# A hybrid decoder step: who issues the recurrence's small loads, and where its triangular solve pauses

## The chip, the cores and the metric

The kernel runs on one core of a Trainium2 chip. The metric is the device time of one execution in microseconds (us); the time of a kernel is the median of its runs.

## The reference

One inference step of a two-layer trunk over a prompt of 16 + 2048 positions and over 8 sequences of 4 new tokens. Layer 0 is sliding-window attention, layer 1 is RWKV-7 time mixing; each has a SiLU gate and a residual, and a last RMSNorm ends the step. The change lies in layer 1, whose core is a recurrence over tokens, for 16 heads with a 64 x 64 state each:

```
def wkv_scan(S0, r, w, k, v, a, b):
    # S_t = S_{t-1} diag(w_t) + (S_{t-1} a_t) b_t^T + v_t k_t^T ;  y_t = S_t r_t
    def step(S, inp):
        r_t, w_t, k_t, v_t, a_t, b_t = inp
        sa = jnp.einsum('bhvk,bhk->bhv', S, a_t)
        S = S * w_t[:, :, None, :] + sa[..., None] * b_t[:, :, None, :] + v_t[..., None] * k_t[:, :, None, :]
        return S, jnp.einsum('bhvk,bhk->bhv', S, r_t)
    S, ys = lax.scan(step, S0, xs)
...
    y = ((y - mean) * lax.rsqrt(var + GN_EPS)).reshape(B, T, R_WIDTH)
    y = y * ln_g.astype(f32) + ln_b.astype(f32)
    y = (y + bonus.reshape(B, T, R_WIDTH)) * jax.nn.silu(g.astype(f32))
    out = jnp.einsum('btw,wd->btd', y.astype(xn.dtype), w_out)
```

## The kernel before

The work stands in three stages: attention, the projections of layer 1, and the recurrence with its output. The change is in the third.

**Units and chunks.** The recurrence goes over units: unit 0 holds the 16 meta tokens (one chunk of 32), units 1 to 16 hold 128 prompt tokens in 4 chunks of 32, and the sample rows come last. Inside a chunk the token-by-token recurrence is turned into matrix products: a small triangular system is solved for every head, and the state moves on once a chunk. `chain` is the serial part of a chunk, in this order: TensorE multiplies Z (the state and the chunk's rows of v) by L into bank C; ScalarE copies the product to `R0s`; TensorE multiplies by `TT`, the inverted triangles (`solve`); ScalarE copies the result into Z; TensorE multiplies Z by the keys `LS`; VectorE scales by the decay products `pe` and writes the next chunk's Z, from which the next chunk's first product is taken.

**What a unit needs two units ahead.** For unit s = u + 2, `scores` makes 32 x 32 triangles on TensorE in two banks, in chunk 1 and in chunk 2 of u. ScalarE copies the triangles out of the banks to `LAs`; VectorE masks the rest of the banks back into `L`. `inverse` then writes `LAs` to a DRAM buffer `la_d`, reads it back with one triangle a row (`LA`), and inverts the triangles column by column on GpSimd: two tensor_tensor, `XT` and `X`, for each of 31 columns j. The result goes out to `tt_d`, and `load_TT` reads it back as `TT`.

**What runs beside it.** `project_out` of unit u - 2 (chunks 0, 1) and `gate` of unit u - 1 (chunks 2, 3) are dense products in steps that fill TensorE between the links of the chain. `outputs` (Y) reads two chunks' Z in one go, in chunk 2 and in chunk 0 of the next unit. `group_norm` is VectorE and ScalarE work with one power on GpSimd (`var`, in chunk 0); `project_out` has one too (`ms`, in chunk 2). 

**Order.** From unit 2 on, `in_order` fixes the order on VectorE, ScalarE and GpSimd as the one in which the program names the instructions; TensorE and SyncE (SP) are ordered by a list scheduler that works with modelled times and priorities. `released` puts a block's instructions behind the last link of the chain on each engine that stands in `anchors`. `inverse` is a generator: at each `yield` it stops, and `steady` takes it on in the next chunk; so its pauses say which GpSimd work of the norms comes between which columns. SP issues nearly all DMAs, in its own order, and stands still before one whose buffer is not free.

**Buffers.** Four Z buffers turn round, chunk by chunk; `pe` and `bont` (decay products and bonus factors of a unit) have four buffers each in the third stage's pool `wk`, which lies where earlier stages had their work tiles; `wp` is a pool that lasts from the second stage to the end.

Of the kernel before, what the change touches and what calls it, by code (L numbers as in the profile page):

```python
# [19 lines left out]
P = 128  # L20
D = 1024
KC = 8
# [8 lines left out]
def tile_hybrid_step(ctx: ExitStack, tc: tile.TileContext, a, o, c):  # L31
# [14 lines left out]
    def stt(out, in0, scalar, in1, op0, op1):  # L46
        v_.scalar_tensor_tensor(out=out, in0=in0, scalar=scalar, in1=in1, op0=op0, op1=op1)  # L47

    def dma(out, in_):
        return nc.sync.dma_start(out=out, in_=in_).ins  # L50

    cst = ctx.enter_context(tc.tile_pool(name="cst", bufs=1))
    dram = ctx.enter_context(tc.tile_pool(name="dram", bufs=1, space=DRAM))
# [889 lines left out]
    def scores(u, c2):  # L943

        nch = u.nch
        mk = smk_s if u.kind == "s" else smk
        w = min(2, nch - 2 * c2)
        L = u.L[c2]

        pss = banks(u)  # L950
        for g in range(KC):
            for cc in range(w):
                for e, ps_ in HS:
                    u.scored = mm(pss[e][64 * cc:64 * cc + 64, g, :], u.BK[g // 4][ps_, g % 4, 2 * c2 + cc, :], L[ps_, e, cc, g, :], True, True)
        for cc in range(w):
            r0 = 64 * cc
            for e in range(2):
                la = u.LAs[32 * (1 - e):32 * (1 - e) + 32, :, 2 * c2 + cc]
                sc = pss[e][r0:r0 + 32, :, 0:32].rearrange("p (h g) i -> p h g i", h=2)
                if u.kind == "s":  # L960
                    for half in range(2):
                        tt(v_, la[:, half], sc[:, half], smk_a[r0:r0 + 32, None, :].broadcast_to([32, 4, 32]), ALU.mult)
                else:
                    act(la, sc)
        for cc in range(w):
            r0 = 64 * cc
            for e in range(2):
                tt(v_, L[OS[e], e, cc], pss[e][r0:r0 + 64], mk[r0:r0 + 64, None, :].broadcast_to([64, KC, 64]), ALU.mult)

    def inverse(u, room=None, ln=None):  # L970

        nch = u.nch
        nl = nch * 16
        la_d = dramr.tile([2, nl // 2, 32, 32], F32, name="la_d", tag=f"la_d{nch}")
        u.tt_d = tt_d = dramr.tile([32, 4, 4 * nch * 32], F32, name="tt_d", tag=f"tt_d{nch}")
        for e in range(2):
            dma(la_d[e].rearrange("l j i -> j l i"),
                u.LAs[32 * e:32 * e + 32].rearrange("p h c g i -> p (h c g) i"))
        eng = v_ if u.idx == 1 else g_
        if u.kind == "m":  # L980
            room = wl.tile([P, 2, 32 * 32], F32, name="roomm", tag="L", bufs=nbuf["L"])
        if room is not None:
            LA = room[:, 0].rearrange("p (j i) -> p j i", i=32)
            XX = room[:, 1].rearrange("p (a k i) -> p a k i", a=2, i=32)
        else:

            LA = wk.tile([P, 32, 32], F32, name="LA", tag="LA", bufs=2)
            XX = None
        if XX is None:
            X = wk.tile([P, 16, 32], F32, name="X", tag="X", bufs=2)  # L990
            XT = wk.tile([P, 16, 32], F32, name="XT", tag="XT")
        else:
            X, XT = XX[:, 0], XX[:, 1]
        if ln is None:
            ln = wp.tile([P, 32], F32, name="ln", tag=("mu", "rst0")[u.idx % 2])
        if nch < 4:
            g_.memset(LA, 0.0)
            g_.memset(ln, 1.0)
        for hh in range(2):
            dma(LA[hh * 64:hh * 64 + nl], la_d.rearrange("e l j i -> (e l) j i"))  # L1000
            dma(ln[hh * 64:hh * 64 + nl], ln_d[u.idx].rearrange("q c g i -> (q c g) i"))
        tt(eng, LA, LA, ln.unsqueeze(2).broadcast_to([P, 32, 32]), ALU.mult)
        dma(X, c["laneid"])

        low = 16 if u.kind == "m" else 0

        part = {2: 16}.get(u.idx, 0)
        cut = [(v_, 0, part), (g_, part, 16)] if 0 < part < 16 else [(v_, 0, 16)] if part else [(eng, 0, 16)]
        for j in range(low, 31):
            if j in (8, 16, 23):  # L1010
                yield
            w = 3 - j % 4 if u.kind == "s" else 31 - j
            for eng, k0, k1 in cut if w else ():
                ks = slice(max(low // 2, k0), min(j // 2 + 1, k1))
                shape = [P, ks.stop - ks.start, w]
                if shape[1] <= 0:
                    continue
                tt(eng, XT[:, ks, :w], LA[:, j:j + 1, j + 1:j + 1 + w].broadcast_to(shape), X[:, ks, j:j + 1].broadcast_to(shape), ALU.mult)
                tt(eng, X[:, ks, j + 1:j + 1 + w], X[:, ks, j + 1:j + 1 + w], XT[:, ks, :w], ALU.add)
        for eng, k0, k1 in reversed(cut):  # L1020
            u.inverted = tt(eng, X[:, k0:k1], X[:, k0:k1], ln[:, None, :].broadcast_to([P, k1 - k0, 32]), ALU.mult)
        for hh in range(2):
            dma(tt_d[hh:32:2].rearrange("k q (l i) -> (q l) k i", i=32), X[hh * 64:hh * 64 + nl])
# [238 lines left out]
    with ExitStack() as ph:  # L1262
# [50 lines left out]
        def small_loads(u):  # L1313
            if u.kind == "s":
                room = wp.tile([P, 192], F32, name="TTs", tag="l1_0")
                u.TT = room[:, 0:128].rearrange("p (c g i) -> p c g i", c=1, i=32)
                u.pe = room[:, 128:192].rearrange("p (g c) -> p g c", c=8)
            else:
                u.pe = wk.tile([P, KC, u.nch], F32, name="pe", tag="pe", bufs=4)
            dma(u.pe, pe_d[u.idx])  # L1320
            if u.kind != "m":
                u.bont = wk.tile([P, 16], F32, name="bont", tag="bont", bufs=4)
                dma(u.bont[:u.n], bo_d[u.idx])

        def new_LAs(u):
# [2 lines left out]
        def load_TT(u):  # L1328
            if u.kind != "s":
                u.TT = wp.tile([P, u.nch, 4, 32], F32, name="TT", tag=("sels", "l2t")[u.idx % 2])  # L1330
            for gh in range(2):
                dma(u.TT[64 * gh:64 * gh + 64].rearrange("p c g i -> p (c g i)"), u.tt_d[:, gh:4:2].rearrange("k q x -> q k x"))
# [17 lines left out]
        anchors = {}  # L1350
        MARK = -1

        def new_Z(u, ch):

            Z = Zs[Zcount[0] % nbuf["Z"]]
            Zcount[0] += 1
            for e in range(2):
                load_v(u, ch, e, Z)
            return Z

        def load_v(u, ch, e, Z):
            b0, r0 = OS[e].start, u.off + ch * 32
            anchors["SP"] = dma(Z[b0 + 32:b0 + 64, e].rearrange("p g d -> p (g d)"), v_d[u.t][r0:r0 + 32, e, :])

        LScount = [0]
        over = []
# [47 lines left out]
        def chain(u, ch):  # L1414
# [15 lines left out]
            anchors["PE"] = m  # L1430
            anchors["ACT"] = act(R0s, C[0][:, 0])

            if ch + 1 < u.nch:
                Zn = new_Z(u, ch + 1)
                u.Z.append(Zn)
            elif u.next is not None:
                Zn = new_Z(u.next, 0)
                u.next.Z.append(Zn)
            else:
                Zn = None  # L1440
# [315 lines left out]
        def steady(i, u, pe):  # L1756
# [9 lines left out]
            for ch in range(4):  # L1766
                if (i, ch) == (2, 0):
                    late_consts()
                rec = chain(u, ch)
                next(rec)  # L1770
                after_rhs()
                if ch in (1, 2):
                    with released():
                        if ch == 1:
                            new_LAs(s)
                        else:
                            outputs(u, 1)
                        scores(s, ch - 1)
                run(pe[ch], 1.2)
                next(rec)  # L1780
                with released():
                    if ch == 0:
                        if i > 2:
                            keys(u, 1)
                        first = L0s.pop(s.idx, None)
                        load_BK(s)
                        s.L.append(first or load_L(s, 0))
                        small_loads(s)
                    if ch == 1:
                        s.L.append(load_L(s, 1))  # L1790
                    if ch == 3:
                        keys(u.next, 0)
                        if i + 3 < len(us):
                            L0s[i + 3] = load_L(us[i + 3], 0)
                        inv[s.idx] = inverse(s)
                        next(inv[s.idx])
                    elif us[i + 1].idx in inv:
                        next(inv[i + 1], None)
                        if ch == 2:
                            load_TT(us[i + 1])  # L1800
# [47 lines left out]
        for i, u in enumerate(us):  # L1848
# [15 lines left out]
            for ch in range(u.nch):  # L1864
# [6 lines left out]
                if i + 1 in inv and i > 1:  # L1871

                    with released():
                        if ch == 0:
                            keys(u, 1)
                        next(inv[i + 1], None)
                        if ch == 2:
                            load_TT(us[i + 1])
                run(ew[ch], 1.2)
                run(pe[ch], VB.get((i, ch), (1.2, 1.9))[0])  # L1880
# [152 lines left out]
```

## Time and profile before

| | |
|---|---|
| time, median of 3 runs | 2533.39 us (2532.25 to 2534.08) |
| the profiled execution | 2542.64 us, its span 2540.9 us |
| busy: PE, DVE, ACT, POOL | 88%, 66%, 46%, 41% |
| stretch 1765.1 to 2341.6 us | 12 units with 4 chunks each: PE busy 487.19 of 576.50 us |

Engines are named as in the profile: PE is TensorE (PEld its weight loads), DVE VectorE, ACT ScalarE, POOL GpSimd, SP SyncE; SPq is SP's queue as it issues a DMA. Rows of a timeline give the start, the busy time, engine, line, operation, names out<-in, shapes and count, and in brackets the idle time of the engine before it with what ended it. `L38`, `L41`, `L44` and `L50` are the helpers for matmul, activation, tensor_tensor and DMA, so groups are told apart by their tiles.

### The profile page before, as it was taken

Reading aid. Unit: us, or ns where it says so; the run is one execution under the profiler, and the core shown is the slowest. Engines: PE = TensorE matmul, PEld = TensorE weight load, DVE = VectorE, ACT = ScalarE, POOL = GpSimd, SP = SyncE. Lnnn points to the kernel's source line nnn. Section 1 sums busy time; section 2 is a strip of 40 time slices with the busy share of each in tenths; the row PEclk is TensorE's granted clock in tenths of the full one; section 3 lists DMA queues with packets and bytes.
Section 4 is the critical chain, followed back from the end, with each engine's and each line's share of the span. In section 5 each row is a group of like instructions: output and inputs, shape, how many; then the busy total and the mean of one; then the engine's idle time right before and its main releaser. Section 6 shows DMA issues by size and latency. Waiting matters only on the chain.

```text
span 2540.9 us, 60840 instructions
## 1 busy us (share of the span) xinstructions
PE 2241.2 (88%) x24932; PEld 1545.2 (61%) x24932; DVE 1676.6 (66%) x3181; ACT 1168.9 (46%) x2799; POOL 1050.7 (41%) x1572
## 2 busy tenths in 40 slices
PE   6999989899999997899999999667888888888897
PEld 5877767667854445477776668345545554555553
DVE  7586683577656987866555666555666676666674
ACT  6676464566432433554433445324445444444431
POOL 4242132233112344443333324324777776777613
PEclk9999998999999998899999999777999999999998
DMA  8433122333247564422222223577355455454423
GB/s 204 127 104 116 60 75 80 109 100 99 87 138 223 196 227 161 137 84 96 88 89 100 88 78 109 146 187 192 104 143 146 119 146 135 121 139 135 103 61 75
DMA packets 346234, 312.97 MB, mean 123 GB/s; under 512 B 205546, under 2 KB 282218, under 8 KB 344131
## 3 DMA queue, kind: packets, MB, share of 16 engines
q1 hardware_dynamic: 344339, 305.30, 41.2%
q0 software_dynamic: 1616, 3.79, 0.7%
q8 instruction: 195, 3.19, 0.5%
q14 instruction: 84, 0.69, 0.1%
HBM read 191.15 MB, written 119.84 MB: 122 GB/s over the span
## 4 chain that ended last, share of the span: by engine, by line
PE 37%; DVE 21%; DMA 15%; ACT 8%; POOL 8%; issue 7%; SPq 4%; POOLq 0%; ACTq 0%; DVEq 0%
PE pd L38 21%; PE po L38 6%; DVE xm L47 5%; SPq L50 4%; PE C L38 3%; DVE xpr L44 2%; DMA TT<-tt_d 2%; DMA BK<-bk 2%; ACT ssb L41 2%; DMA tt_d<-X 2%; POOL X L44 2%; PE pz L38 2%; DMA wst<-in_rwkv_w_in 2%; PE sc L38 1%; POOL XT L44 1%
## 5 line engine op out<-in xcount | busy, mean ns | idle before, releaser
L38 PEld LDWEIGHTS <-yp 128*128 128x128 f16 x1488 | 142.3, 100 | 167.4 <-issue 16.5
L47 DVE SCALAR_TENSOR_TENSOR xm<-dx,mu,xn 128x256 f32<-128x256 f32 (+2 forms) x432 | 200.1, 523 | 49.9 <-POOL dx L44 48.5
L44 POOL TENSOR_TENSOR X<-X,XT 128x126 f32<-128x126 f32 (+24 forms) x458 | 200.9, 439 | 35.6
L44 POOL TENSOR_TENSOR XT<-LA,X 128x126 f32<-128x126 f32 (+24 forms) x458 | 183.6, 401 | 36.2 <-issue 2.5
L38 PE MATMUL pd<-xp,wq 128*128 128x256 f16 (+2 forms) x1728 | 186.1, 266 | 11.8 <-DVE qp L47 8.0
L38 PE MATMUL pd<-wg,xg 128*128 128x512 f16 (+1 forms) x816 | 193.3, 384 | 0.4 <-DMA xg<-xg 0.4
L38 PE MATMUL po<-wo,yp 128*128 128x512 f16 x768 | 193.3, 395 | 0.0
L38 PE MATMUL pd<-xp,wg 128*128 128x256 f16 (+2 forms) x1728 | 187.4, 270 | 0.8 <-DVE xp L44 0.4
L38 PE MATMUL pd<-wvv,xpr 128*128 128x512 f16 (+1 forms) x816 | 186.6, 386 | 0.0
L38 PE MATMUL pd<-xpr,w 128*128 128x256 f16 (+2 forms) x1728 | 186.5, 267 | 0.0
L38 PEld LDWEIGHTS <-wq 128*128 128x128 f16 x1728 | 159.4, 99 | 33.2 <-DVE qp L47 9.2
L38 PE MATMUL pd<-xpr,wkk 128*128 128x256 f16 (+2 forms) x1728 | 179.5, 264 | 0.0
L44 POOL TENSOR_TENSOR ssb<-ssb,bias 128x512 f32<-128x512 f32 x64 | 86.3, 1355 | 222.7 <-DVE ssb L462 181.4
L38 PEld LDWEIGHTS <-wg 128*128 128x128 f16 x1728 | 161.7, 100 | 24.0 <-issue 3.9
L38 PEld LDWEIGHTS <-w 128*128 128x128 f16 x1728 | 157.8, 99 | 27.2 <-issue 9.7
L38 PEld LDWEIGHTS <-wkk 128*128 128x128 f16 x1728 | 158.2, 98 | 15.6 <-issue 0.4
L38 PE MATMUL pd<-w,yp 128*128 128x512 f16 x720 | 162.2, 383 | 3.5 <-DMA yp<-y 3.5
L44 POOL TENSOR_TENSOR ps<-wst,ps 128x1024 f16<-128x1024 f32 x32 | 69.4, 2170 | 226.8 <-ACT wst L41 208.3
L44 DVE TENSOR_TENSOR L<-pz,smk 64x512 f32<-64x512 f32 x128 | 88.1, 689 | 96.7 <-ACT LAs L41 94.7
L38 PEld LDWEIGHTS <-xpr 128*128 128x128 f16 (+1 forms) x816 | 78.8, 100 | 102.1 <-issue 16.4
L44 DVE TENSOR_TENSOR xpr<-xm,xpr 128x512 f16<-128x512 f32 (+2 forms) x144 | 99.0, 709 | 56.7 <-ACT xpr L41 56.3
L41 ACT ACTIVATE ssb<-ssb,ng 128x128 f32<-128x128 f32 (+1 forms) x272 | 104.2, 384 | 57.3 <-DVE es L44 53.6
(357 smaller groups left out, 4715.4 us busy)
## 6 DMA issues: line engine op xcount, KB each, us to landing
wst<-in_rwkv_w_in SPq DMA_DIRECT2D x32, 512.0 KB
wsp<-ps SPq DMA_DIRECT2D x32, 512.0 KB
BK<-bk SPq DMA_DIRECT2D x32, 512.0 KB
L<-ar SPq DMA_DIRECT2D x64, 256.0 KB
x<-in_x_prompt SPq DMA_DIRECT2D x29, 512.0 KB
xn<-xn SPq DMA_DIRECT2D x14, 1028.0 KB
ar<-aro SPq DMA_DIRECT2D x28, 512.0 KB
bk<-bko SPq DMA_DIRECT2D x28, 512.0 KB
```

What stands on the lines that cost most here:

```text
L38: return t_.matmul(out=out, lhsT=lhsT, rhs=rhs, start=start, stop=stop, **kw).ins
L41: return s_.activation(out=out, in_=in_, func=func, **kw).ins
L44: return e.tensor_tensor(out=out, in0=in0, in1=in1, op=op).ins
L47: v_.scalar_tensor_tensor(out=out, in0=in0, scalar=scalar, in1=in1, op0=op0, op1=op1)
L50: return nc.sync.dma_start(out=out, in_=in_).ins
```

## The change

It does six things.

1. `dma` can be given the engine that issues. `inverse` has `la_d <- LAs` (two DMAs a unit) issued by ScalarE.
2. `inverse` pauses once more, right behind these two DMAs. In `steady` it is now begun in chunk 2, right behind `scores`, and taken on in chunk 3, where it was begun before.
3. The column loop pauses at j = 8, 18, 23 and 27 (before: 8, 16, 23). The added piece, columns 23 to 26, is named in chunk 2 ahead of `after_rhs`, in which the `ms` power of `project_out` lies; the last one stays where it was.
4. For units 2 to 14 the two loads of the next chunk's rows of v are issued by ScalarE, right behind `R0s`; these no longer renew the SP anchor.
5. In `scores` the copies and the masks go bank by bank (both chunks of bank 0, then both of bank 1), not chunk by chunk.
6. `pe` and `bont` are taken from `wp`, no longer from `wk`.

```
-    def dma(out, in_):
-        return nc.sync.dma_start(out=out, in_=in_).ins
+    def dma(out, in_, eng=None):
+        return (eng or nc.sync).dma_start(out=out, in_=in_).ins
...                                                  # scores, twice: copies, then masks
-        for cc in range(w):
-            r0 = 64 * cc
-            for e in range(2):
+        for e in range(2):
+            for cc in range(w):
+                r0 = 64 * cc
...                                                  # inverse
             dma(la_d[e].rearrange("l j i -> j l i"),
-                u.LAs[32 * e:32 * e + 32].rearrange("p h c g i -> p (h c g) i"))
+                u.LAs[32 * e:32 * e + 32].rearrange("p h c g i -> p (h c g) i"), s_)
+        yield
...
-            if j in (8, 16, 23):
+            if j in (8, 18, 23, 27):
                 yield
...                                                  # small_loads
-                u.pe = wk.tile([P, KC, u.nch], F32, name="pe", tag="pe", bufs=4)
+                u.pe = wp.tile([P, KC, u.nch], F32, name="pe", tag="pe", bufs=4)
-                u.bont = wk.tile([P, 16], F32, name="bont", tag="bont", bufs=4)
+                u.bont = wp.tile([P, 16], F32, name="bont", tag="bont", bufs=4)
...                                                  # load_v (new_Z hands eng on)
-            anchors["SP"] = dma(Z[b0 + 32:b0 + 64, e].rearrange("p g d -> p (g d)"), v_d[u.t][r0:r0 + 32, e, :])
+            x = dma(Z[b0 + 32:b0 + 64, e].rearrange("p g d -> p (g d)"), v_d[u.t][r0:r0 + 32, e, :], eng)
+            if eng is None:
+                anchors["SP"] = x
...                                                  # chain, behind R0s
+            eng = s_ if 1 < u.idx < len(us) - 2 else None
             if ch + 1 < u.nch:
-                Zn = new_Z(u, ch + 1)
+                Zn = new_Z(u, ch + 1, eng)
...                                                  # steady
                 next(rec)
+                if ch == 2:
+                    with released():
+                        next(inv.get(i + 1, idle()), None)
                 after_rhs()
...
                         scores(s, ch - 1)
+                        if ch == 2:
+                            inv[s.idx] = inverse(s)
+                            next(inv[s.idx])
...
-                        inv[s.idx] = inverse(s)
                         next(inv[s.idx])
...                                                  # unit 15, outside steady
                         next(inv[i + 1], None)
                         if ch == 2:
+                            next(inv[i + 1], None)
                             load_TT(us[i + 1])
```

More of the change, by code (lines that the diff above doesn't have):

```diff
@@ L964, in scores @@
                     act(la, sc)
-        for cc in range(w):
-            r0 = 64 * cc
-            for e in range(2):
+        for e in range(2):
+            for cc in range(w):
+                r0 = 64 * cc
                 tt(v_, L[OS[e], e, cc], pss[e][r0:r0 + 64], mk[r0:r0 + 64, None, :].broadcast_to([64, KC, 64]), ALU.mult)
@@ L1351, in tile_hybrid_step, with new_Z @@
         MARK = -1
-        def new_Z(u, ch):
+        def new_Z(u, ch, eng=None):
             Z = Zs[Zcount[0] % nbuf["Z"]]
@@ L1357, in new_Z, with load_v @@
             for e in range(2):
-                load_v(u, ch, e, Z)
+                load_v(u, ch, e, Z, eng)
             return Z
-        def load_v(u, ch, e, Z):
+        def load_v(u, ch, e, Z, eng=None):
             b0, r0 = OS[e].start, u.off + ch * 32
-            anchors["SP"] = dma(Z[b0 + 32:b0 + 64, e].rearrange("p g d -> p (g d)"), v_d[u.t][r0:r0 + 32, e, :])
+            x = dma(Z[b0 + 32:b0 + 64, e].rearrange("p g d -> p (g d)"), v_d[u.t][r0:r0 + 32, e, :], eng)
+            if eng is None:
+                anchors["SP"] = x
         LScount = [0]
@@ L1431, in chain @@
             anchors["ACT"] = act(R0s, C[0][:, 0])
+            eng = s_ if 1 < u.idx < len(us) - 2 else None
             if ch + 1 < u.nch:
-                Zn = new_Z(u, ch + 1)
+                Zn = new_Z(u, ch + 1, eng)
                 u.Z.append(Zn)
             elif u.next is not None:
-                Zn = new_Z(u.next, 0)
+                Zn = new_Z(u.next, 0, eng)
                 u.next.Z.append(Zn)
```

## The prediction

> **What bounds the kernel now.** I read the page first, then the busy times by stretch, then who waits for whom in the recurrence, and last one unit of it in order of time.
>
> ```profile
> span 2540.9 us, 60840 instructions
> PE 37%; DVE 21%; DMA 15%; ACT 8%; POOL 8%; issue 7%; SPq 4%; POOLq 0%; ACTq 0%; DVEq 0%
> ```
>
> The chain that ended last is mostly PE, but over a third of it lies on DVE, DMAs and POOL: a stage is bound by latencies. All of the change but its sixth point and the small reorderings in `scores` and `inverse` acts in units 2 to 14. I take the stretch from the first chunk of unit 3 to that of unit 15; below, 24 issues of `la_d` at two a unit show that it holds 12 units.
>
> ```profile
> 1765.10:2341.60 576.50, 487.19 (x9136) 296.77 (x9127) 380.06 (x601) 254.61 (x648) 414.95 (x840) 0.95 0.52 133
> PE C L38 <- issue: 45.6, 32, 3.4
> PE C L38 <- DMA TT<-tt_d: 24.2, 14, 2.5
> PE pz L38 <- DMA BK<-bk: 3.5, 7, 0.8
> POOL LA L44 <- DMA LA<-la_d: 71.4, 13, 32.2
> POOL var L1613 <- DVE var L1610: 31.0, 11, 4.3
> POOL ms L1694 <- ACT po L41: 30.2, 11, 4.8
> ACT yp L41 <- PE yps L1663: 85.4, 24, 5.9
> ACT LAs L41 <- PE pz L38: 22.6, 20, 2.4
> SPq L50 <- PE Y L38: 206.9, 13, 19.6
> ```
>
> The first row is one stretch (time, then busy PE, PEld, DVE, ACT, POOL, then clock, DMA share, GB/s), the others are waits (total, times, longest). A unit takes 576.5/12 = 48.04 us. PE is busy for 40.6 of it and idle for 7.4, of which three pieces concern the change: 45.6 before the first product of a chunk (C from Z and L, which waits for DVE's four writes of Z), 24.2 before the solve, which waits for `TT`, and 3.5 before the scores for `BK`. One unit shows what stands behind them:
>
> ```profile
> 1887.42 0.60 ACT L41 ACTIVATE po<-h 128x512 f32<-128x512 f32 x1
> 1888.22 0.19 POOL L1694 TENSOR_SCALAR ms<-ssq 128x2 f32<-128x2 f32 x1 [2.53 <-ACT po L41]
> 1889.30 0.37 POOL L44 TENSOR_TENSOR XT<-LA,X 128x96 f32<-128x96 f32 x1
> 1890.56 1.55 ACT L41 ACTIVATE LAs<-pz 32x256 f32<-32x256 f32 x4 [2.42 <-PE pz L38]
> 1891.74 2.79 DVE L44 TENSOR_TENSOR L<-pz,smk 64x512 f32<-64x512 f32 x4 [4.74 <-ACT LAs L41]
> 1892.13 1.71 SPq L50 DMA_DIRECT2D la_d<-LAs  x2
> 1892.56 1.56 ACT L41 ACTIVATE Z<-C 32x256 f32<-32x256 f32 x4 [0.46 <-PE C L38]
> 1892.75 0.28 POOL L44 TENSOR_TENSOR XT<-LA,X 128x56 f32<-128x56 f32 x1
> 1894.48 1.15 PE L38 MATMUL C<-Z,LS 128*64 128x64 f32 x32
> 1897.26 1.73 DVE L44 TENSOR_TENSOR Z<-C,pe 64x256 f32<-64x256 f32 x4
> 1899.09 0.65 PE L38 MATMUL C<-Z,L 128*32 128x64 f32 x32 [1.41 <-issue]
> 1900.78 1.91 POOL L44 TENSOR_TENSOR LA<-LA,ln 128x1024 f32<-128x1024 f32 x1 [2.43 <-DMA LA<-la_d]
> 1920.38 0.20 POOL L1613 TENSOR_SCALAR var<-var 128x16 f32<-128x16 f32 x1 [2.14 <-DVE var L1610]
> ```
>
> And the way of the triangles, from the chain of waits:
>
> ```profile
> 1864.22 0.95 PE C L38 x28
> 1946.10 4.90 DMA tt_d<-X
> 1951.65 7.54 DMA TT<-tt_d
> 1959.23 0.64 PE C L38 x28
> ```
>
> This is a loop over two units. From one unit's solve (1864.22) to the last copy to `LAs` in its chunk 2 (1890.56 + 1.55 = 1892.11) go 27.9 us; to GpSimd's first multiply of the triangles (1900.78) 8.7; from there to the end of the inverse (about 1945.4, right ahead of `tt_d`) 44.6; out, back in and to the solve (1959.23) 13.8. Together 95.0, half of it 47.5: that is the unit time, and `TT` ends it. GpSimd is busy for 414.95/12 = 34.6 of 48.04 us, so it is not its work but its waits that count: inside the 44.6 it stands 2.14 us before `var` and 2.53 before `ms`, on average (31.0 + 30.2)/12 = 5.1.
>
> **The change part by part.**
>
> *Solve in five pieces.* Columns 16 and 17 go ahead of `var`, columns 23 to 26 ahead of `ms`. The four columns take 1892.75 - 1889.30 = 3.45 us and cover the 2.53 before `ms`; `ms` itself then runs 0.9 late, and its reader on DVE is named a chunk later, so nothing waits. Two columns are half as many, some 1.8 us, and cover most of the 2.14 before `var`, which is 0 to 0.3 late. So the inverse shrinks by about 4.4, to 40.2, and the loop to 27.9 + 8.7 + 40.2 + 13.8 = 90.6, or 45.3 a unit. Without its waits for `TT` PE needs 48.04 - 24.2/12 = 46.0, and with the other gains below 45.2. So `TT` no longer leads, but what is late next, PE's own order and the writes of Z, is just as late. As the two loops lie within a tenth and single units differ by more, I count 0.7 of the 24.2: 17.0 us. Ends: 0 and 24.2.
>
> A rule speaks against it, in the Trainium skill's page "SBUF — State Buffer" (rules for DVE and GpSimd run concurrently): when a VectorE operation with two SBUF inputs and a GpSimd one meet, the second to issue blocks until the first has finished. The trace agrees:
>
> ```profile
> 1881.96 1.23 DVE L44 TENSOR_TENSOR ytm<-ytm,var 128x1024 f32<-128x1024 f32 x1
> 1882.07 1.36 POOL L44 TENSOR_TENSOR XT<-LA,X 128x110 f32<-128x110 f32 x1
> 1884.84 0.39 POOL L44 TENSOR_TENSOR XT<-LA,X 128x108 f32<-128x108 f32 x1
> ```
>
> beside `ytm` a step takes 1.36 instead of 0.39 us. By that rule the six moved columns, were each caught once, would give back 6 x 0.97 = 5.8 us, and the gain of the part would be none. I don't take it, since they move into stretches in which DVE reads banks (Z from C, reductions of Y).
>
> *Triangles' way out by ScalarE.* The two issues leave SP and stand on ACT between the copies to `LAs` and the copies to Z.
>
> ```profile
> L50 SPq DMA_DIRECT2D la_d<-LAs x24: 457/563/1592, 1797.2 to 2326.1; - x24
> L50 SPq DMA_DIRECT2D Z<-v x96: 302/419/1821, 1766.3 to 2323.4; - x96
> ```
>
> No DMA is issued by ACT in this trace; the nearest rows are SP's (shortest, median, longest in ns), and I take the medians, with the longest as the bad end. Two issues are 1.13 us. In the unit shown ACT was free of `LAs` at 1892.11 and began Z at 1892.56, so Z comes 0.68 late, and LS with it. But LS ended at 1895.6 and DVE wrote Z from 1897.26, held by its own queue: 1.6 us of cover, 1.2 once the masks are earlier (next). So it costs nothing here; without the cover, 0.68 x 12 = 8 us. In the unit shown SP issued at once (1892.13), so the way itself isn't shorter; units in which SP was held gain up to a longest issue, 1.6. I take 0.
>
> *Masks bank by bank.* DVE's first mask began at 1891.74, right behind the third of ACT's four copies, which is the last of its bank; with one bank's copies first it follows the second, 1.55/4 = 0.39 earlier. DVE's queue runs on without a gap into the writes of Z, and these into the next chunk's product, 1.4 us of idle PE in the unit shown. So chunk 2 gains 0.39 x 12 = 4.7. Chunk 1 has the same masks; there the loads of v (next) take part of it.
>
> *Rows of v by ScalarE.* Eight issues a unit, two behind each `R0s`: 0.84 us. In chunks 0 and 3 ACT next waits for PE's transposes (yps, 85.4/24 = 3.6 each); in chunk 2 for the scores, 2.42 in the row above; over chunks 1 and 2 together that wait is 22.6/24 = 0.94 on average, so chunk 1 is the tight one. I take 1.8 of its 4.7 as lost: 2.9 stay (ends -5 and +4.7). No wait comes with it: of the four Z buffers the one to be filled was last read by Y a chunk or more before. What SP is rid of is more than the issues: it stood 206.9 us, 17 a unit, before loads of v whose buffer Y still read, with `L` and `BK` queued behind. `BK` comes two to four issues of 0.42 earlier, so of the 3.5 before the scores I count 2.0.
>
> *Decay products in places of their own.* This acts where the recurrence starts:
>
> ```profile
> 1651.28 0.42 SPq L50 DMA_DIRECT2D pe<-pe  x1
> 1652.28 1.11 SPq L50 DMA_DIRECT2D TT<-tt_d  x2
> 1660.92 1.73 DVE L44 TENSOR_TENSOR Z<-C,pe 64x256 f32<-64x256 f32 x4 [7.88 <-DMA pe<-pe]
> 1662.75 1.08 PE L38 MATMUL C<-Z,L 128*32 128x64 f32 x32 [11.26 <-issue]
> ```
>
> The first unit's `pe`, named long before, is issued at 1651.28, when its place is free, and DVE stands 7.88 us for it. With a place of its own that goes. Late next is `TT` of unit 1, issued at 1652.28 and one us earlier then; with the 7.54 of the row above it lands near 1660. PE has dense steps and transposes to fill that. I take half of 7.88: 4.0 (ends 0 and 7.9).
>
> The sum: 17.0 + 4.7 + 2.9 + 2.0 + 4.0 = 30.6 us less than the profiled execution's 2542.6 (its span of 2540.9 and 1.7 around it). The median of the runs shown is 9.2 lower, 2533.4; the same saving gives 2502.8, say 2503.
>
> **The rivals.** *The wait only moves to SP's queue (2520).* `LA` and `TT` are still issued by SP, in the scheduler's order, and no anchor holds its loads any more. If `LA` of the next unit gets behind `TT`, which waits 4.90 us for `tt_d`, GpSimd starts later by about what its pieces save. Against it: in the trace `LA` goes first. The 17.0 would be gone: 2533.4 - 13.6.
>
> *The change doesn't do what it says (2533).* The chain is held by DVE (45.6 us before a chunk's first product, nearly twice what `TT` has), and what the solve gains is waited off there, while PE's order, laid anew, costs the rest.
>
> *Slower: ACT's issues come into the chain (2556).* With t us an issue, a unit is exposed by 2t - 0.94 in chunk 1, 2t - 2.42 in chunk 2 ahead of `LAs`, and 2t - 0.45 - 1.0 behind it, each from zero up. At the medians that is nothing to speak of; at t = 1.5, just under the longest rows, 2.1 + 0.6 + 1.6 = 4.2 a unit, 50 us, against 27.7 gained beside it (the sum without chunk 1's 2.9): 22 slower. It decides from 27.7/12 = 2.3 a unit, at t = 1.17. For it: SP's longest are 1.6 to 1.8 and DMAs are busy for 0.52 of the time; against it: the medians.
>
> *Slower: rows of v land late (2545).* They used to be issued ahead by SP; now their issue follows `R0s`, and the next chunk's first product, right ahead of the next `R0s`, reads them.
>
> ```profile
> 1946.27 0.38 ACT L41 ACTIVATE R0s<-C 128x256 f32<-128x256 f32 x1 [1.11 <-PE C L38]
> 1955.89 0.38 ACT L41 ACTIVATE R0s<-C 128x256 f32<-128x256 f32 x1
> ```
>
> That short chunk has 9.62 us; less 0.84 for the issues and half a us for the product they have 8.3, against 7.54 for the longer of the DMAs above. Each us beyond costs up to three chunks a unit, 36 us. The Trainium skill's page "DMA: Bandwidth & Descriptors" (rules for kernel authors) says that spreading DMAs over issuing engines doesn't help bandwidth and only saves the sequencer's time. By that rule the landing is no sooner on ACT's queue and the sum stays as it is; no row here shows a DMA of ACT's.
>
> **How the numbers follow.** Forecast 0.58, its own range 2486 (24.2 + 9.4 + 3.5 + 7.9 gained, and 2 more from SP) to 2517; `LA` behind `TT` 0.15; no effect 0.10; ACT's issues 0.13; late v 0.04. The range reaches from 2486 to 2537: it leaves out the slower cases and a few of the fastest, about 0.2. What a measurement here can tell from no change is about 0.2%, 5 us. Faster than that: the first two, 0.73. Within: most of the third, 0.07. Slower: 0.20.
>
> **What would show it.** Right: the solve's wait for `TT` under 8 us in a stretch of 12 units, GpSimd's waits before `var` and `ms` near 10 and 0, DVE's first mask behind ACT's second copy, ACT's issues near 0.42 and 0.56, and no 7.88 before the first Z. Wrong: `TT` still waited for with `LA` issued later (the first rival); PE waiting for Z longer than 45.6; ACT's idle time before Z filled by issues of over a us; a chunk's first product released by the loads of v.

## The result, and the profile after

The changed kernel takes 2558.7 us (median of four runs) against 2533.7 for the kernel before on the same chip: ratio 1.0101, 95% interval 1.0082 to 1.0121. It is slower by 1%, 22 us above the range forecast.

Where the time lies is read from the starts of ACT's `R0s`, one a chunk. Up to unit 1 the changed kernel is 18.5 us ahead; unit 1 takes back 12.0 and unit 2, whose first solve stands 17.9 us for `TT` (0.9 before), another 9.2; the twelve units 3 to 14, the steady stretch, take 594.3 us instead of 576.5, that is 17.8 more; what follows is 5.6 shorter. Together +14.9, the difference of the two spans (2555.8 and 2540.9).

The mean length of a chunk in that stretch, with the granted TensorE clock of the chunk in brackets, and the times of all kernels run (e1 and so on are told of below). Each ratio is against the kernel before, run on the same chip beside it, where its median was 2533.7 to 2538.0 us. One of e14's four executions took 3701.6 us at a granted clock of 0.556 and is left out of its time.

| kernel | time, us | ratio to before | chunk 0 | chunk 1 | chunk 2 | chunk 3 |
|---|---|---|---|---|---|---|
| before | 2533.7 | 1 | 14.97 (0.91) | 10.99 (0.97) | 11.63 (0.99) | 10.45 (0.96) |
| after | 2558.7 | 1.0101 (1.0082 to 1.0121) | 12.89 (0.90) | 10.53 (1.00) | 12.05 (1.00) | 14.05 (0.92) |
| e1 v by SP | 2559.9 | 1.0085 (1.0053 to 1.0117) | 12.85 (0.91) | 10.06 (1.00) | 11.37 (1.00) | 15.03 (0.91) |
| e2 v by SP, no anchor | 2549.1 | 1.0051 (1.0036 to 1.0067) | 12.89 (0.91) | 10.05 (1.00) | 11.41 (1.00) | 14.56 (0.92) |
| e3 after, TT in four | 2509.6 | 0.9889 (0.9860 to 0.9918) | 11.93 (1.00) | 10.72 (1.00) | 11.71 (1.00) | 11.92 (0.96) |
| e4 before, TT in four | 2490.4 | 0.9826 (0.9778 to 0.9875) | 11.91 (0.99) | 10.67 (0.99) | 11.54 (1.00) | 10.50 (0.96) |
| e5 before, pieces | 2611.1 | 1.0308 (1.0267 to 1.0348) | 13.00 (0.90) | 10.63 (0.99) | 11.96 (0.98) | 19.00 (0.81) |
| e6 before, v by ACT | 2572.3 | 1.0159 (1.0132 to 1.0186) | 13.46 (0.99) | 13.75 (0.83) | 11.70 (1.00) | 11.16 (0.99) |
| e7 = e3, v by SP | 2525.4 | 0.9958 (0.9938 to 0.9978) | 12.78 (0.92) | 9.99 (1.00) | 11.10 (1.00) | 13.76 (0.96) |
| e8 = e7, la_d by SP | 2522.6 | 0.9955 (0.9937 to 0.9972) | 12.74 (0.92) | 10.33 (0.99) | 11.30 (1.00) | 13.23 (0.96) |
| e9 after, vt first | 2537.9 | 1.0011 (0.9999 to 1.0022) | 11.99 (1.00) | 13.36 (0.85) | 12.06 (1.00) | 10.30 (0.94) |
| e10 before, TT by columns | 2540.6 | 1.0017 (1.0004 to 1.0031) | 13.37 (0.97) | 13.17 (0.85) | 11.75 (0.99) | 10.42 (0.96) |
| e11 = e4, masks, places | 2473.4 | 0.9756 (0.9737 to 0.9775) | 11.93 (0.99) | 10.33 (0.98) | 11.14 (1.00) | 10.58 (0.99) |
| e12 = e8, vt first | 2522.3 | 0.9947 (0.9930 to 0.9964) | 12.80 (0.91) | 10.45 (1.00) | 11.20 (0.99) | 13.29 (0.96) |
| e13 = e12, tt_d behind vt | 2497.8 | 0.9849 (0.9823 to 0.9875) | 13.28 (0.96) | 10.33 (0.99) | 11.60 (0.99) | 10.47 (0.94) |
| e14 = e13, v and la_d by ACT | 2503.0 | 0.9884 (0.9850 to 0.9918) | 12.57 (0.98) | 11.04 (0.95) | 12.21 (0.99) | 10.43 (0.94) |
| e15 = e11 again | 2475.8 | 0.9770 (0.9745 to 0.9796) | 11.89 (0.99) | 10.46 (0.99) | 11.14 (1.00) | 10.74 (1.00) |

So the gain came (chunk 0 is 2.08 us shorter, chunk 1 0.46) and was given back in chunk 3, 3.60 a unit, and in chunk 2, 0.42. The waits of the changed kernel over the same twelve units, after a row of the stretch itself:

```profile
1767.90:2362.20 594.30, 485.56 (x9138) 300.53 (x9129) 384.16 (x602) 256.81 (x648) 392.87 (x835) 0.95 0.51 129
PE C L38 <- issue: 77.3, 40, 4.3
PE C L38 <- DVE Z L44: 13.8, 3, 5.0
DVE vt L44 <- DMA vt<-v: 52.6, 12, 5.2
ACT yp L41 <- DMA Z<-v: 33.0, 11, 4.7
ACT Z L41 <- issue: 14.4, 7, 2.7
POOL LA L44 <- DMA LA<-la_d: 57.4, 8, 8.5
POOL var L1617 <- DVE var L1614: 32.6, 11, 3.8
POOL ms L1698 <- ACT po L41: 23.0, 12, 2.6
```

PE's wait for `TT` (24.2) and for `BK` (3.5) are gone from the list. PE's wait before a chunk's first product has grown from 45.6 to 77.3 + 13.8; nearly all of the growth lies in chunk 3, where it went from 2.2 to 44.3. DVE's wait for `vt`, now once in each unit, is seven times what it was; the row of the kernel before is:

```profile
DVE vt L44 <- DMA vt<-v: 7.5, 8, 1.9
```

ACT's wait before its own loads of v is new. One chunk 3 in order of time:

```profile
1899.65 1.17 SPq L50 DMA_DIRECT2D LA<-la_d  x2
1900.93 1.08 SPq L50 DMA_DIRECT2D TT<-tt_d  x2
1902.06 0.91 SPq L50 DMA_DIRECT2D vt<-v  x2
1902.43 2.28 ACTq L50 DMA_DIRECT2D Z<-v  x2
1904.53 1.91 POOL L44 TENSOR_TENSOR LA<-LA,ln 128x1024 f32<-128x1024 f32 x1 [7.09 <-DMA LA<-la_d]
1905.00 0.60 ACT L41 ACTIVATE yp<-yps 128x512 f16<-128x512 f32 x1 [2.20 <-DMA Z<-v]
1908.13 1.15 PE L38 MATMUL C<-Z,LS 128*64 128x64 f32 x32
1912.08 1.49 DVE L44 TENSOR_TENSOR vt<-vt,bont 128x512 f32<-128x512 f32 x2 [4.95 <-DMA vt<-v]
1913.48 1.72 DVE L44 TENSOR_TENSOR Z<-C,pe 64x256 f32<-64x256 f32 x4
1915.30 0.65 PE L38 MATMUL C<-Z,L 128*32 128x64 f32 x32 [3.97 <-issue]
```

`vt` is the norm's copy of v, multiplied by `bont` on DVE ahead of the writes of Z, in DVE's fixed order. It is loaded in chunk 3 from SP's queue. Before, SP issued it ahead of `TT`:

```profile
1899.82 2.34 SPq L50 DMA_DIRECT2D vt<-v  x2
1903.40 1.12 SPq L50 DMA_DIRECT2D TT<-tt_d  x2
```

Now `TT` goes first, at 1900.93, `vt` at 1902.06, and it lands at about 1912, 10 us later (on average DVE starts on it 9.5 us after its issue, before the change 4.6). DVE stands 4.95 us for it; LS was through at 1909.3, and Z is written from 1913.5. PE stands 3.97.

That stand is paid twice. The next rows are of two microseconds each; the numbers behind the last bracket are the granted clock, the busy share of the 16 DMA engines and GB/s:

```profile
1912.00:1914.00 2.00, 0.00 (x0) 0.00 (x0) 1.91 (x4) 0.00 (x0) 1.76 (x4) 1.00 0.12 49
1916.00:1918.00 2.00, 2.00 (x94) 1.76 (x83) 0.76 (x1) 0.39 (x1) 1.77 (x4) 0.59 0.80 254
1918.00:1920.00 2.00, 2.00 (x15) 1.25 (x8) 0.12 (x1) 0.72 (x2) 1.69 (x5) 0.55 0.99 218
```

Right behind the stand PE's clock falls, in chunk 0, which is dense: the two rows have 0.59 and 0.55 as means, and the clock's own record has one half for 3.41 us from 1916.38. That is why chunk 0 has 0.90 in the table although its solve waits for nothing any longer.

Why the load takes 10 us is in the DMA row of the page for a window (40 slices, mean busy share of the 16 DMA engines in tenths): the changed kernel at 1900 to 1915, and then e3, in which `TT` is cut in another way, at 1879 to 1894, each from about `TT`'s issue:

```profile
DMA  5033998999798976489712111999511111111000
```

```profile
DMA  9199999999989993116999686039859843799999
```

In the first the row ends in a long tail of ones; the row of 1912 to 1914 above has it as 0.12 of sixteen engines, which is two. It is `TT`, whose two DMAs have 2 as their outermost dimension. What is issued behind it on the queue has its packets on those two engines behind `TT`'s. The packets show it: of the 128 of the store of `h`, issued at 1908.59, 112 go between 1909.4 and 1910.7 and the last 16, two engines' share of sixteen, from 1912.6 to 1914.0. In the second row the tail is gone. This is a rule of the Trainium skill, page "DMA: Bandwidth & Descriptors", section "Rules for kernel authors": an outermost dimension of c < 16 keeps a DMA on at most c engines. The trace agrees (0.12 of 16).

### The profile page after: what moved, and what is told of

Same layout as the page of the kernel before. It is cut to its first block, busy times and chain, and to the rows that moved or that the text cites. A ratio compares the mean times of both kernels' runs of the same rounds, so it can differ in the third digit from the quotient of the medians.

```text
span 2555.8 us, 60802 instructions
## 1 busy us (share of the span) xinstructions
PE 2231.9 (87%) x24932; PEld 1545.1 (60%) x24932; DVE 1675.1 (66%) x3181; ACT 1170.9 (46%) x2799; POOL 1028.7 (40%) x1572
## 4 chain that ended last, share of the span: by engine, by line
PE 49%; DVE 19%; issue 9%; DMA 8%; ACT 8%; POOL 5%; SPq 2%; ACTq 0%; POOLq 0%; DVEq 0%
PE pd L38 27%; PE po L38 7%; PE C L38 5%; DVE xm L47 4%; DVE xpr L44 2%; SPq L50 2%; PE pz L38 2%; PE sc L38 2%; ACT ssb L41 1%; PE Y L38 1%; DMA wst<-in_rwkv_w_in 1%; DMA vt<-v 1%; PE kt L1383 1%; PE oT L38 1%; DMA TT<-tt_d 1%
## 5 line engine op out<-in xcount | busy, mean ns | idle before, releaser
L44 POOL TENSOR_TENSOR X<-X,XT 128x126 f32<-128x126 f32 (+24 forms) x458 | 185.2, 404 | 35.7
L38 PE MATMUL po<-wo,yp 128*128 128x512 f16 x768 | 185.8, 384 | 0.0
L38 PE MATMUL C<-Z,L 128*32 128x64 f32 x2048 | 48.7, 243 | 115.9 <-issue 89.2
```

Source lines behind the costliest of these rows:

```text
L38: return t_.matmul(out=out, lhsT=lhsT, rhs=rhs, start=start, stop=stop, **kw).ins
L44: return e.tensor_tensor(out=out, in0=in0, in1=in1, op=op).ins
```

## The experiments

Theory S: SP's queue. The earlier end of the solve lets `TT` (and `tt_d`) go ahead of loads that DVE or PE need sooner; `TT` on two engines then holds them. Theory A: ACT, which is in order, stands before its own DMA issues, and this lengthens chunks 2 and 3.

**e1, e2: the rows of v issued by SP again**, once with and once without renewing SP's anchor.

```
-            eng = s_ if 1 < u.idx < len(us) - 2 else None
+            eng = None                                                # e1
+            eng = nc.sync if 1 < u.idx < len(us) - 2 else None        # e2
```

> The changed kernel with the rows of v issued by SP again (point 4 undone, the other points kept). Theory A (ACT, in order, stands before its own DMA issues, which is what lengthens chunks 2 and 3): ACT's stall of some 3 us a unit in the second half goes, and DVE's stand for vt goes with it, since the order on SP is the one of the kernel before; 2505 to 2520 us. Theory S (TT's load stands ahead of vt on SP's queue and holds it): if TT stays ahead of vt, vt still lands 10 us after its issue, DVE stands about 4 us before chunk 3's Z, and the time is 2545 to 2560.

> The changed kernel with the rows of v of units 2 to 14 issued by SP, but without their being the anchor of SP's order, so that of point 4 only what it does to the order is left. Theory A: ACT doesn't issue them, so its stands before the second rows of v go: 2505 to 2530 us. Theory S with the anchor as the cause of the order: TT goes ahead of vt as in the changed kernel, DVE stands about 4 us before chunk 3's Z, 2545 to 2560 us.

Measured: 2559.9 and 2549.1, both in the range of S. Nearly all of ACT's stands go, chunk 1 is 0.5 us and chunk 2 0.65 shorter than in the changed kernel, and in chunk 3 1.0 us of that (e1) and 0.5 (e2) is lost again, since DVE stands longer for `vt` (61.6 us in e1, up to 9.1 at once). A is a cost of some 1.1 us a unit in chunks 1 and 2, but not what ended chunk 3. `TT` goes ahead of `vt` in all twelve units of both runs, so the anchor isn't the cause of the order.

**e3, e4, e10: the cut of TT.** Same bytes, same places; e3 is the changed kernel, e4 the kernel before, e10 the kernel before with four DMAs that keep the outermost 2.

```
-                dma(u.TT[64 * gh:64 * gh + 64].rearrange("p c g i -> p (c g i)"), u.tt_d[:, gh:4:2].rearrange("k q x -> q k x"))
...                                                  # e3, e4: outermost 32
+                for q in range(2):
+                    r0 = 64 * gh + 32 * q
+                    dma(u.TT[r0:r0 + 32].rearrange("p c g i -> p (c g i)"), u.tt_d[:, gh + 2 * q])
...                                                  # e10, in their place: outermost 2, half the columns
+                for q in range(2):
+                    h = 64 * u.nch; c0 = h * q
+                    dma(u.TT[64 * gh:64 * gh + 64].rearrange("p c g i -> p (c g i)")[:, c0:c0 + h], u.tt_d[:, gh:4:2, c0:c0 + h].rearrange("k q x -> q k x"))
```

> The changed kernel with TT loaded by four DMAs of 32 partitions each in place of two whose outermost dimension is 2. Theory S (vt lands late because TT's packets, on two of the sixteen DMA engines, are ahead of it): TT lands in about 3 us, vt lands within 6.3 us of its issue as before the change, DVE's stand before Z in chunk 3 goes (some 3.6 us a unit over 14 units): 2505 to 2530 us. Theory A: the stall is at ACT's issues and not with TT: about 2555 us, as the changed kernel.

> The kernel before with TT loaded by four DMAs in the same way, nothing else. If the 24.2 us for which PE waits for TT in twelve units are the time of TT's two-engine transfer, most of it goes: 2510 to 2520 us. If they are the time of the steps ahead of the issue, TT's issue stays the end of the path and the time stays at 2530 to 2535 us.

> The kernel before with TT in four DMAs that keep the outermost dimension of 2 (each of 64 partitions and half the columns), as a control for the run with four DMAs of 32 partitions. If it is the spread over DMA engines that made that run 1.7% faster: no gain, 2530 to 2545 us (smaller packets may cost a little). If it is the number of DMAs: about 2490 us.

Measured: 2509.6, 2490.4 and 2540.6. e3 lies in the range of S, e10 in that of the spread, and e4 gained 20 us more than its 2510 to 2520. It is the spread, not the number of DMAs. In e3 DVE's wait for `vt` falls from 52.6 to 2.5, though `TT` is still issued first:

```profile
DVE vt L44 <- DMA vt<-v: 2.5, 8, 0.5
ACT yp L41 <- DMA Z<-v: 47.6, 9, 7.4
```

and chunk 3 is still longer than e4's (11.92 against 10.50). The waits put that down to ACT's stands, now uncovered: PE waits 16.4 us for ACT's copies to Z, which e4 doesn't have. That A is next is the reading of these rows; no run takes ACT's stands away and leaves SP's queue as it is (e7, below, lays it anew). In e4 chunk 0 is 3.06 us shorter, half as much again as the wait for `TT` (24.2/12 = 2.0): the rest is the clock, 0.99 in place of 0.91, by the table. A chunk 0 of the kernel before and one of e4:

```profile
1955.90:1971.50 15.60, 12.19 (x200) 7.23 (x192) 9.22 (x16) 6.54 (x17) 10.96 (x22) 0.89 0.74 189
```

```profile
1929.40:1941.10 11.70, 10.18 (x195) 6.34 (x188) 9.06 (x16) 6.50 (x16) 10.04 (x22) 1.00 0.89 235
```

The same work keeps PE busy for 12.19 us and for 10.18. In e10 the wait for `TT` only halves, and another takes its place: PE's for `BK`, 3.5 before.

```profile
PE pz L38 <- DMA BK<-bk: 20.5, 19, 2.4
PE C L38 <- DMA TT<-tt_d: 12.5, 9, 1.9
```

**e5: the pieces alone**, on the kernel before.

```
-            if j in (8, 16, 23):
+            if j in (8, 18, 23, 27):
...          # and one more next(inv[i + 1]) in chunk 2, ahead of after_rhs
```

> The kernel before with the solve in five pieces alone (pieces end at columns 8, 18, 23 and 27, one more piece ahead of the scores in chunk 2; triangles, v, masks and decay products as before). Theory S: with tt_d ready earlier, SP issues TT ahead of vt, so PE's wait for TT in chunk 0 goes (chunk 0 from 15.0 to about 12.9 us) and DVE stands about 4 us for vt in chunk 3 (10.5 to 14 us or more): 2540 to 2565 us. Rival: the pieces are innocent, the wait for vt comes of another point: 2505 to 2520 us.

Measured: 2611.1. As S says, but larger, and outside the range of either: `tt_d` is also pulled ahead of the second `la_d` (and `TT` ahead of `LA`, as the first rival of the prediction had it), SP stands for the end of the inverse with `la_d`, `LA` and `vt` behind it, and everything of the next unit comes later.

```profile
DVE vt L44 <- DMA vt<-v: 99.0, 12, 11.0
POOL LA L44 <- DMA LA<-la_d: 217.9, 13, 32.0
```

So point 3, of which I expected most of the gain, costs 3% by itself; with the rest of the change two thirds of that are won back.

**e6: rows of v by ACT alone**, on the kernel before (the diff's lines in `load_v`, `new_Z` and `chain`).

> The kernel before with point 4 alone (rows of v of units 2 to 14 issued by ScalarE). Theory A as a second, smaller cost: ACT stands before the second of its two issues where an earlier DMA of SP's has not landed, in chunks 2 and 3 mostly, 1 to 1.5 us a unit over 13 units, and nothing is gained: 2540 to 2560 us. If ACT's issues lie beside other work: 2530 to 2536 us.

Measured: 2572.3, above both ranges and beyond what ACT's stands explain (chunks 2 and 3 are 0.07 and 0.71 longer); chunk 1 is 2.76 longer. Without its Z loads SP's queue is laid anew:

```profile
2013.49 1.09 SPq L50 DMA_DIRECT2D TT<-tt_d  x2
2014.63 0.43 SPq L50 DMA_DIRECT2D out_y_prompt<-h  x1
2022.77 0.32 SPq L50 DMA_DIRECT2D h<-h  x1
...
2025.38 2.23 SPq L50 DMA_DIRECT2D L<-ar  x2
2027.71 2.27 SPq L50 DMA_DIRECT2D BK<-bk  x2
```

The store of `h` goes out right behind `TT`; the load into the same `h` waits 7 us for that store on SP, and `bont`, `pe`, `xg` (the rows left out) and `L` now stand ahead of `BK`, which the scores need in chunk 1.

```profile
PE pz L38 <- issue: 21.7, 13, 3.7
PE pz L38 <- DMA BK<-bk: 8.9, 10, 2.4
```

These were 3.8 and 3.5 before. In chunk 1 the "issue" of the first row is `BK` too: in nine of the twelve units PE begins the scores 0.09 us after the first of its two loads has landed. Neither theory had named `BK`; it is S's mechanism with another load at its end.

**e9: vt ahead of TT** in the changed kernel, the one swap on SP's queue.

```
                         next(inv[i + 1], None)
-                        if ch == 2:
-                            load_TT(us[i + 1])
...                      # chunk 3, behind the norm's loads; u.vt_ld is the last of them
+                    if us[i + 1].idx in inv:
+                        with released(), tc.issue_after(u.vt_ld):
+                            load_TT(us[i + 1])
```

> The changed kernel, with one swap on SP's queue and nothing else: the two loads of vt stand ahead of the two of TT in every steady unit, as in the kernel before. Theory S (DVE stands before chunk 3's Z because vt is issued behind TT's wait for tt_d and behind its slow packets): DVE's stand for vt (46.9 us in ten units) goes to under 10, chunk 3 comes from 14.05 to about 11 us, TT still lands before chunk 0's right-hand sides: 2505 to 2520 us. Rival (ACT's stands before its issues are what lengthens chunk 3, the wait for vt only overlaps them): 2545 to 2560 us.

Measured: 2537.9, short of S's 2505 to 2520. Chunk 3 comes to 10.30 and chunk 0 to 11.99 at full clock, as S says, and DVE's wait for `vt` is gone, so that wait was the cause of both; but chunk 1 goes to 13.36:

```profile
PE pz L38 <- DMA BK<-bk: 27.0, 19, 3.6
```

The wait has moved on to `BK`, as in e6. In each of the orders tried with `TT` on two engines (before, after, e1, e2, e5, e6, e9, e10) PE or DVE stands for `TT` itself or for a load behind it; the order chose which.

**e7, e8, e12: the whole change with TT in four, issues back on SP.** e7 is e3 with v by SP, e8 has `la_d` by SP too, e12 is e8 with `vt` ahead of `TT`.

> The changed kernel with TT in four DMAs and the rows of v issued by SP again. Theory A: the 1.4 us by which chunk 3 of the changed kernel with TT in four DMAs is longer than that of the kernel before with TT in four DMAs (11.9 against 10.5) is ACT standing before its issues of v, and goes: 2485 to 2497 us. If the rows of v cost nothing: 2505 to 2514 us as with them on ACT.

> The same with la_d issued by SP again as well: what is left of the change is the masks, the pieces and the decay products' places. If la_d's issue by ACT costs something of its own (1.6 to 2.3 us before the first copy of chunk 3's Z), 2475 to 2487 us; if not, as the run with only v back. If pieces, masks and places bring anything once TT's transfer is short, below the 2490 us of the kernel before with TT in four DMAs; if the pieces only moved the wait for TT, the same 2490.

> The changed kernel with v and la_d issued by SP, TT in four DMAs and vt ahead of TT: the whole change but its ACT issues, with the queue mended. Against the same kernel with TT ahead of vt (2523 us, DVE standing 35 us for vt in eleven units): theory S says 2482 to 2495 us, and if the five pieces bring anything beyond the short TT, under the 2490 of the kernel before with TT in four DMAs. Rival: a stand of another load takes the place of vt's, 2510 to 2525 us.

Measured: 2525.4, 2522.6 and 2522.3. What A expected of e7 fell, the other range named for it too, and so did what S expected of e12; e8 is the same as e7 within their scatter, so `la_d`'s issue by ACT costs nothing that shows. e12 has the rival's time, but the stand is still `vt`'s. Giving v back to SP makes e3 slower by 16 us: in chunk 3 loads of v and `pe` now come ahead of `vt` on SP's queue, DVE stands 55.7 us for it, and the chunk grows from 11.92 to 13.76. e12 turned out to change little: in e8 `TT` stood ahead of only the second of `vt`'s two loads in eleven of the twelve units. In e12 both are ahead of `TT`, and DVE stands 39.0 us all the same:

```profile
DVE vt L44 <- DMA vt<-v: 39.0, 11, 5.0
SPq L50 <- POOL X L44: 36.9, 11, 5.0
```

SP stands 36.9 for `X` (the end of the inverse, for `tt_d`; 7.5 in e4), with `LA` and `vt` behind: measured from the end of chunk 3's `R0s`, `vt` is issued at 3.04 us on average, in e4 at 1.08.

**e11, e15: masks and places with TT in four**, no pieces, v and `la_d` by SP as before.

> The kernel before with TT in four DMAs of 32 partitions, the masks bank by bank and the decay products in places of their own; pieces, la_d and v as before. The terms of the prediction that depend on no queue: masks 4.7 in chunk 2 and 4.7 in chunk 1 over twelve units, BK 2.0 and the start's 4.0 at most, so 2475 to 2485 us beside the 2490 of the kernel before with TT in four DMAs. Rival: these waits were beside PE's own work, 2487 to 2495 us.

> The kernel with TT in four DMAs, masks and places once more, on the same chip as the two with the order kept, for the comparison with them: 2468 to 2480 us.

Measured: 2473.4 and 2475.8, 2.3 to 2.4% faster than the kernel before. Against e4 chunk 1 is 0.34 us and chunk 2 0.40 shorter, together 8.9 us over twelve units (in e15, the same kernel, 0.21 and 0.40). Nothing that the places brought can be seen to stay: unit 1 starts 6.8 us sooner than in e4 and lasts 6.1 longer. No run has the places alone.

```profile
1746.00:2273.80 527.80, 468.15 (x9137) 283.19 (x9132) 384.59 (x600) 254.68 (x648) 415.77 (x843) 0.99 0.57 146
```

**e13, e14: the whole change, `TT` in four, with the queue mended.** `inverse` yields ahead of `tt_d`, and `tt_d` and `TT` are named behind `vt` in chunk 3; e13 issues v and `la_d` by SP, e14 by ACT.

```
+        yield
         for hh in range(2):
             dma(tt_d[hh:32:2]...
...                      # chunk 3; the lines around it are e9's
                         with released(), tc.issue_after(u.vt_ld):
+                            next(inv[i + 1], None)
                             load_TT(us[i + 1])
...                      # unit 15, outside steady: one more next(inv[i + 1], None)
```

> The whole change but its ACT issues, TT in four DMAs, and SP's order as in the kernel before: tt_d and TT are issued behind LA and vt (a yield ahead of tt_d in the solve, taken in chunk 3 after vt's loads). It differs from the kernel with masks and places (2473 us) only in the pieces. If the pieces cost what they cost by pulling tt_d ahead of LA and vt on SP's queue: back to 2465 to 2480 us, DVE's stand for vt under 15 us in eleven units. If the pieces cost something on POOL or elsewhere: 2500 to 2525 us, as with tt_d ahead.

> The same with v and la_d issued by ScalarE: the whole change with the queue mended. Theory A alone is left then: ACT's stands before its own issues in chunks 2 and 3, 1 to 1.5 us a unit, 2480 to 2500 us. If a shorter SP queue is worth more than ACT's stands: 2455 to 2470 us.

Measured: 2497.8 and 2503.0. The first lies between what the two explanations gave (2465 to 2480 for the queue, 2500 to 2525 for GpSimd or another place), the second 3 us above the 2480 to 2500 of theory A. Half of it held: chunk 3 comes back from e12's 13.29 to 10.47, with DVE's wait for `vt` at 1.0, so the pieces' cost there came by the queue and not by GpSimd. But `tt_d` behind `vt` now lands late itself:

```profile
PE C L38 <- DMA TT<-tt_d: 10.4, 9, 2.9
SPq L50 <- DMA tt_d<-X: 58.0, 12, 6.2
POOL var L1620 <- DVE var L1617: 0.5, 2, 0.3
POOL ms L1701 <- ACT po L41: 1.4, 3, 0.5
```

GpSimd's waits before `var` and `ms` are gone, and chunk 0 is 1.4 us longer than in e11 all the same. With `TT` short, PE waits for it in none of e11's twelve units, so there is nothing for the pieces to win. Against e13, e14 is 0.71 longer in chunk 1 and 0.61 in chunk 2, the cost of ACT's issues, but 0.71 shorter in chunk 0, so that a unit is 0.6 longer. Whether yet another order would have the pieces for nothing stays open.

## Why the prediction was wrong

- **The step that failed: the solve in five pieces, 17.0 us.** I worked out what the earlier end of the inverse is worth on the loop's own way and did not go along SP's queue to see what `tt_d` and `TT`, coming earlier, are issued ahead of. The gain on the way was real: `TT`'s wait went from 24.2 to nothing. The wait for `vt` that it caused is 52.6 us in the same twelve units (7.5 before), and with it goes the clock. e5 has the pieces alone: 3% slower, `TT` ahead of `vt` in all twelve units. My first rival named this queue, but only `LA` behind `TT`; the load that mattered was `vt`, whose reader stands ahead of the writes of Z. One of the signs of being wrong came, PE waiting for Z longer than 45.6; as in the second rival, the gain was waited off at DVE, but DVE stood there for a load.
- **A term that was taken as fixed.** The loop of 95.0 us held `TT`'s 7.54 us as given. It was the shortest way to the same gain: e4 gets 1.7%, some 44 us, from those few lines. I quoted the row and didn't ask why a DMA of 128 KB takes 7.5 us.
- **PE's busy time was taken as fixed.** I wrote that PE needs 46.0 us a unit without its waits for `TT`. It needs less, since the wait slows what follows: 487.2 us of busy time in the stretch before, 466.5 in e4. The clock's record has one half for 54.6 us of the stretch before and for 15.4 of e4's; half of the difference, 19.6, is nearly all of the 20.7 (an estimate, with all work at half speed in that time). Each microsecond of PE's wait for `TT` was worth about 1.5 in chunk 0 (3.06 gained for 2.0).
- **"No wait comes with it", rows of v by ACT.** The issues themselves are as forecast: 0.32 and 0.57 us in the median, against 0.42 and 0.56. But ACT stands before them, up to 4.7 us:

```profile
L50 ACTq DMA_DIRECT2D Z<-v x96: 308/320/1522, 1768.0 to 2349.8; - x96
L50 ACTq DMA_DIRECT2D la_d<-LAs x24: 322/569/2272, 1795.1 to 2341.6; - x24
```

  It isn't the Z buffer, as I had argued, but a semaphore: in the program's waits the DMAs of SP and ACT take eight semaphores in turn, and one that is to use a semaphore again waits until the DMA that used it has landed. In the chunk shown, ACT's second load of v goes when `LA`, a load of SP's, has landed (GpSimd starts on it at 1904.53). It is so in eleven of the twelve units: the load goes 0.02 us after the second `LA` has landed, whose semaphore it takes, and 1.3 to 4.4 us after ACT was free. So the third rival was right that ACT's issues come into the chain, but priced them by their length; in chunks 1 and 2 they cost 1.1 (e1) to 1.3 (e14) us a unit by the wait. That its 2556 lies near the 2558.7 measured is chance: e1, in which SP issues v, takes 2559.9.
- **SP rid of loads, BK sooner.** The change took `BK`'s 3.5 away, as forecast (2.0). Alone, the same point made `BK` late (e6): what a queue is rid of lets others move up.
- **Masks bank by bank** was right: DVE's first mask starts 0.36 us before ACT's third copy ends, and chunks 1 and 2 are shorter by 4.1 and 4.8 us over twelve units (e11 against e4; e15 has 2.5 and 4.8), where I had 4.7 each without the loads of v.
- **Places of their own.** The stand of 7.88 us before the first Z is gone, as forecast, and that Z is written 18 us sooner (1642.87 in place of 1660.92). Unit 2 starts 6.5 us sooner in the changed kernel, forecast 4.0, but then stands 17.9 for its `TT`, and e11 against e4 has only 0.7 left at that point. So the wait went and the gain of 4.0 is not shown; that 6.5 is of its size is chance.
- **GpSimd's waits.** I expected 10 and 0 before `var` and `ms`; they are 32.6 and 23.0. With ACT's loads of v taken away they are 18.3 and 5.3 (e1), and 0.5 and 1.4 with the queue in order (e13): the work ahead of both is ACT's (squares, and its copies of `po`), which comes late when ACT stands. The inverse takes 44.8 us on average before, 42.5 after and 38.4 in e13 (forecast 40.2); e11, without the pieces, has 40.8.
- **The blocking of GpSimd by VectorE** was weighed against the part and left out, because the moved columns would run while DVE reads banks. For one of the six that was wrong. In the changed kernel column 23 runs beside `ytm`:

```profile
1884.96 1.24 POOL L44 TENSOR_TENSOR XT<-LA,X 128x96 f32<-128x96 f32 x1
1886.02 1.27 DVE L44 TENSOR_TENSOR ytm<-ytm,lng 128x1024 f32<-128x1024 f32 x1
1886.28 1.25 POOL L44 TENSOR_TENSOR X<-X,XT 128x96 f32<-128x96 f32 x1
```

  Its two steps took 0.37 and 0.38 us on average before and take 1.16 and 1.17 now; the six columns together went from 4.7 to 6.3 us a unit, so 1.6 was given back, where the prediction had 5.8 if each were caught once. The columns that stood beside such work before got shorter, so that all 31 together fell from 26.8 to 25.1. In e13 the six are at 4.8.

## What to carry to other kernels

Before a step is brought forward, follow every DMA that it issues along its queue: what it now goes ahead of, and who reads that. Look at how a transfer is cut before working around its time: a tail of ones in the DMA row can say that few engines carry it, as it did here. And a wait on the path can cost more than its length when TensorE stands in it, here 1.5 times.

## What the runs showed of the hardware

- **A DMA with outermost dimension 2 runs on two engines** and holds what is behind it on the queue: `vt` landed 10 us after its issue behind it, and DVE's wait for it went from 52.6 to 2.5 us with the same bytes in rows of 32 partitions.
- **The clock falls after a short stand.** A stand of 3.97 us was followed by 3.41 us at one half. In the kernel before, 2.34 us of idle PE before the solve (from 1956.9) were enough for 3.41 us at one half from 1959.96:

```profile
1960.00:1962.00 2.00, 2.00 (x8) 1.11 (x7) 0.53 (x1) 1.11 (x3) 1.69 (x5) 0.50 0.39 86
1962.00:1964.00 2.00, 2.00 (x11) 1.25 (x10) 1.97 (x4) 1.09 (x4) 1.69 (x5) 0.66 0.95 285
```

  The Trainium skill's page "TensorE: Matmul & The Clock Gate" (section "Part 1: The HAM clock gate") has the clock at half after an idle window of about 3.4 us. The first stand agrees. The second is shorter than that window and still cost the clock, so here the measurement decides: a gap of 2.3 us among sparse small products can be enough. It is no single case: of the fourteen falls of the clock in the stretch of the kernel before, thirteen follow gaps of at most 3.03 us, and the least are gaps of 1.24 and 0.55 us close together. Each time the clock was at one half for 3.41 us or twice that.
- **Issues on two engines aren't independent** in this program, whose DMAs take eight semaphores in turn. ACT's loads of v waited for the landing of SP's `LA`, 1.3 to 4.4 us in eleven of twelve units.
